# Strassen steps for five of eleven gate/up pairs, and a feed-forward in four interleaved parts

## The chip, the core and the metric

The program runs on one core of one Trainium2 chip. The metric is the device time of one execution in microseconds (us). TensorE (PE in the profile) multiplies, VectorE (DVE), ScalarE (ACT) and GpSimd (POOL) compute elementwise, and SyncE (SP) issues the loads. Each engine works through its own list of instructions in order; semaphores make one engine wait for another.

## The reference, cut to what matters

One transformer layer with 256 rows and a model width of 2048 in float32. Attention, retention and gates come first and are not touched by the change. What follows them is the feed-forward:

```python
h2 = rms_norm(x, g_ffn)
g, u = jnp.split(h2 @ w_ffn_in, 2, axis=-1)     # w_ffn_in: 2048 x 11264, gate and up halves of 5632
return x + (jax.nn.silu(g) * u) @ w_ffn_out     # w_ffn_out: 5632 x 2048
```

## The kernel before, in words

Activations are stationary in TensorE (128 rows of K on the partitions, 128 tokens as columns), and the weights stream past them 512 columns at a time. The 256 tokens are two blocks of 128. Every float32 operand is split into two parts, hi and lo, in the type float32r; a product is three matmuls, hi by hi, hi by lo and lo by hi (`mm3`, L85 to L89).

The weights are one long stream. A *chunk* is 512 columns of a weight matrix over all of K, and adds into two PSUM banks, one for each token block (tag `pm`, four banks, so that one chunk's pair can be emptied while the next chunk's fills). A *group* is two tiles of 128 rows of K of a chunk: 2 tiles x 2 token blocks x 3 = 12 matmuls. For a group, ACT writes the hi part of 128 x 1024 weights (`wh`, L79) and DVE subtracts it from the raw weights to get the lo part (`wl`, L80). Hi and lo have four buffers each, and the split of a group stands three groups ahead of its matmuls (`SPLIT_AHEAD`). A raw tile (`raw`, 1 MB, three buffers) holds two groups; SP issues its load (L135) when a buffer comes free, and that is when DVE has subtracted the last group in it.

When a chunk ends, it is evacuated. A gate chunk goes through ACT's Silu (L544), an up chunk through two DVE instructions that multiply it by the gate (L552). The hidden block is then transposed by DVE in 16 STREAM_TRANSPOSE instructions and split in two halves; `later` spreads these over the next eight groups (L277 to L290).

The feed-forward is eleven pairs of a gate and an up chunk (16 tiles of K each). After six of them come four chunks of `w_ffn_out` (w_fo) over the hidden width made so far, after the other five four more (L592 to L598). All of it is written in program order; the Tile scheduler fixes, before the run, the order of the instructions on each engine and which buffer a tile gets.

Of the kernel before, what the change touches and what calls it, by code (L numbers as in the profile page):

```python
# [39 lines left out]
def hybrid_layer_kernel(ctx, tc, xt, x, w_in, w_oa, w_or, w_out, qg, kg, gm, gf, w_fi, w_fo, out):  # L40
    """One token block of 256 rows through the layer.

    Every float32 operand of a product is split exactly into two parts of 12 significant bits
    (float32r), and a product is hi*hi + hi*lo + lo*hi in float32 accumulation. Activations are
    stationary (K on partitions), weights stream past them 512 columns at a time. RMS scales
    multiply the products' rows, gains multiply the transposed activations' rows. VectorE transposes
    activations in 32 x 32 blocks, which leaves TensorE to the products.
    """
# [42 lines left out]
    def rsqrt(a, w):  # L91
        """1/sqrt(a), with a Newton step after the table's square root; a is overwritten."""
# [11 lines left out]
    chunks = []  # L104
    groups = []

    def add_chunk(w, cols, kts, lhs, evac, before=None):
        ci = len(chunks)
        chunks.append(dict(w=w, cols=cols, kts=kts, lhs=lhs, evac=evac, before=before))
        j = 0  # L110
        while j < len(kts):
            # The first tiles are small, so that the products start early.
            n = 1 if ci == 0 and j < FIRST else SPLIT_KT
            i = j - j % LOAD_KT
            groups.append(dict(c=ci, first=(j == 0), last=(j + n >= len(kts)), load=i, off=j - i, n=n, j=j))
            j += n

    raws = {}

    def emit_load(g):  # L120
        G = groups[g]
        C = chunks[G["c"]]
        key = (G["c"], G["load"])
        if key in raws:
            return
        kts = C["kts"][G["load"]:G["load"] + LOAD_KT]
        t = wp.tile([P, LOAD_KT, NC], F32, tag="raw", bufs=3, name=nm("raw"))
        step = groups[g]["n"] if G["c"] == 0 else LOAD_KT
        for k in range(0, len(kts), step):
            kk = kts[k:k + step]  # L130
            n = len(kk)
            c0 = 0
            for a, ln in C["cols"]:
                src = C["w"][kk[0] * P:(kk[0] + n) * P, a:a + ln].rearrange("(k p) n -> p k n", p=P)
                nc.sync.dma_start(t[:, k:k + n, c0:c0 + ln], src)  # L135
                c0 += ln
            if G["c"] == 0:
                load_xt(G["load"] + k, n)
        raws[key] = t

    parts = {}

    def emit_split(g):
        G = groups[g]
        t = raws[(G["c"], G["load"])]
        hi = wp.tile([P, SPLIT_KT, NC], F32R, tag="hi", bufs=SPLIT_AHEAD + 1, name=nm("wh"))
        lo = wp.tile([P, SPLIT_KT, NC], F32R, tag="lo", bufs=SPLIT_AHEAD + 1, name=nm("wl"))
        n = G["n"]
        split(hi[:, 0:n, :], lo[:, 0:n, :], t[:, G["off"]:G["off"] + n, :])
        parts[g] = (hi, lo)  # L150

    acc = {}

    def emit_mm(g):
        G = groups[g]
        C = chunks[G["c"]]
        if G["first"]:
            acc[G["c"]] = [ps.tile([P, NC], F32, tag="pm", bufs=4, name=nm("pm")) for _ in range(NB)]
        hi, lo = parts.pop(g)
        n = G["n"]  # L160
        for b in range(NB):
            o = acc[G["c"]][b]
            bs = slice(b * P, (b + 1) * P)
            for i in range(n):
                lh, ll = C["lhs"](C["kts"][G["j"] + i])
                mm3(o, (lh[:, bs], ll[:, bs]), (hi[:, i, :], lo[:, i, :]),
                    start=G["first"] and i == 0, stop=G["last"] and i == n - 1)
# [21 lines left out]
    # Idle work while the first tiles come in: ScalarE's table, TensorE's clock.  # L189
# [37 lines left out]
    def build_consts():  # L227
# [4 lines left out]
        # rel[p, :128] = p - j in the first block of rows, rel[p, 128:] = 128 + p - j in the second.  # L232
# [6 lines left out]
        # dec[j, h, i] = exp(log_g[h] * (i - j)) for i >= j, else 0.  # L239
# [420 lines left out]
```

## Time and profile before

| | us |
|---|---|
| median of 3 runs (1545.41 to 1546.79) | 1546.36 |
| span of the profiled execution | 1543.8 |
| median less the span (what lies around it) | 2.6 |
| TensorE busy | 1535.9 |
| VectorE busy | 1045.1 |
| ScalarE busy | 723.2 |

The span runs from the first to the last instruction of the profiled execution; its own time as a run is not listed, so the difference from the median stands for what lies around it. The busy times are sums of instruction durations. An engine that is busy all the time is the first candidate for what sets the end, but whether the others keep up is read stage by stage.

### The profile page before, as it was taken

The page shows a single profiled execution, that of the slowest core. Times are in us where ns is not written, and L with a number is a line of the kernel's source. Part 1 is how long each engine was busy: PE and PEld are TensorE (multiplying, and loading weights), DVE is VectorE, ACT ScalarE, POOL GpSimd, SP SyncE. Part 2 cuts the span into 40 slices and gives each one's busy share as a digit, 9 for nine tenths or more (in the row PEclk, how much of TensorE's full clock was granted, in tenths as well). Part 3 has the DMA queues.
Part 4 walks back from the last instruction along what each step waited for, and adds up shares of the span by engine and source line. Part 5 has one row for each costly group of instructions (what it writes and reads, how often), then busy time and mean ns, then how long its engine had stood idle before and what let it go on. Part 6 is the DMA issues. An engine that isn't in the chain of part 4 may idle for free.

```text
span 1543.8 us, 17497 instructions
## 1 busy us (share of the span) xinstructions
PE 1535.9 (99%) x6837; PEld 1270.3 (82%) x6837; DVE 1045.1 (68%) x1424; ACT 723.2 (47%) x827; POOL 21.1 (1%) x28
## 2 busy tenths in 40 slices
PE   9999999999999999999999999999999999999998
PEld 6788888888888888888888888888888888888887
DVE  7989868777764747474998666666744466666743
ACT  7565554545454444444455444444433444444432
POOL 1101000000000000000000000000000000000000
PEclk9999999999999999999999999999999999999999
DMA  9455555565566555566556655655656555655663
GB/s 351 167 191 163 171 183 192 164 197 185 173 199 196 195 191 191 191 210 228 189 192 197 204 185 194 201 191 191 192 192 196 196 185 193 209 192 191 204 204 109
DMA packets 157907, 298.95 MB, mean 194 GB/s; under 512 B 5216, under 2 KB 22144, under 8 KB 157568
## 3 DMA queue, kind: packets, MB, share of 16 engines
q1 hardware_dynamic: 157696, 297.82, 58.4%
q8 instruction: 53, 0.87, 0.2%
q14 instruction: 30, 0.25, 0.0%
q0 software_dynamic: 128, 0.02, 0.0%
HBM read 295.72 MB, written 2.10 MB: 193 GB/s over the span
## 4 chain that ended last, share of the span: by engine, by line
PE 98%; DVE 1%; DMA 0%; issue 0%; ACT 0%; SPq 0%; ACTq 0%; DVEq 0%
PE pm L88 32%; PE pm L89 32%; PE pm L87 32%; PE sd L88 1%; PE sd L89 1%; PE sd L87 0%; DVE e L290 0%; DVE wl L80 0%; DMA raw<-in_w_in 0%; PE sd L372 0%; SPq L205 0%; SPq L135 0%; ACT L95 0%; ACT wh L79 0%; DVE e L569 0%
## 5 line engine op out<-in xcount | busy, mean ns | idle before, releaser
L80 DVE TENSOR_TENSOR wl<-raw,wh 128x1024 fp32r<-128x1024 f32 (+1 forms) x554 | 673.9, 1220 | 448.8 <-ACT wh L79 444.9
L79 ACT ACTIVATE wh<-raw 128x1024 fp32r<-128x1024 f32 (+1 forms) x554 | 583.3, 1056 | 685.4 <-PE pm L89 660.7
L87 PE MATMUL pm<-wh,u 128*128 128x512 f32 x2208 | 860.3, 390 | 1.5 <-ACT u L82 0.8
L88 PE MATMUL pm<-wl,u 128*128 128x512 f32 x2208 | 859.2, 389 | 1.2 <-DVE wl L80 1.1
L89 PE MATMUL pm<-wh,u 128*128 128x512 f32 x2208 | 859.1, 389 | 0.0
L87 PEld LDWEIGHTS pm<-wh,u 128*128 128x128 f32 x2208 | 414.5, 188 | 89.0 <-ACT u L82 2.6
L88 PEld LDWEIGHTS pm<-wl,u 128*128 128x128 f32 x2208 | 414.6, 188 | 87.4 <-DVE wl L80 2.1
L89 PEld LDWEIGHTS pm<-wh,u 128*128 128x128 f32 x2208 | 414.5, 188 | 86.3 <-DVE u L83 0.2
L290 DVE STREAM_TRANSPOSE e<-e 32x256 f32<-32x256 f32 x432 | 188.3, 436 | 11.4 <-ACT e L400 3.9
L79 ACT ACTIVATE u<-e 128x512 fp32r<-128x512 f32 x50 | 29.0, 625 | 49.9 <-DVE e L290 49.9
L80 DVE TENSOR_TENSOR u<-e,u 128x512 fp32r<-128x512 f32 x50 | 32.7, 691 | 0.5 <-ACT u L79 0.5
L290 DVE STREAM_TRANSPOSE e<-u 32x256 f32<-32x256 f32 x64 | 27.9, 436 | 1.3
L544 ACT ACTIVATE e<-pm,rstd 128x512 f32<-128x512 f32 x22 | 15.1, 690 | 9.3 <-PE pm L89 9.2
L344 POOL TENSOR_SCALAR e<-rel 128x384 f32<-128x384 f32 x8 | 14.1, 1766 | 114.9 <-PE sd L372 33.9
L552 DVE SCALAR_TENSOR_TENSOR e<-pm,rstd,e 128x512 f32<-128x512 f32 x22 | 15.4, 743 | 0.0
L82 ACT ACTIVATE u<-e,g_ffn 128x256 fp32r<-128x256 f32 x16 | 7.2, 498 | 15.1 <-DVE e L290 15.1
L475 ACT ACTIVATE e<-pm,rstd 128x512 f32<-128x512 f32 x16 | 10.9, 690 | 6.6 <-PE pm L89 6.6
L569 DVE TENSOR_TENSOR e<-pm,u 128x512 f32<-128x512 f32 x8 | 5.2, 684 | 7.9 <-PE pm L89 7.9
L95 ACT ACT_TABLE_LOAD x8 | 10.3, 1283 | 0.1
L483 DVE TENSOR_TENSOR e<-pm,e 128x512 f32<-128x512 f32 x16 | 10.2, 682 | 0.0
L362 ACT ACTIVATE e<-e,s 128x128 f32<-128x128 f32 (+1 forms) x16 | 7.2, 448 | 5.4 <-DVE s L359 5.4
L460 DVE TENSOR_TENSOR e<-e,e 128x1024 f32<-128x1024 f32 x4 | 4.9, 1224 | 5.7 <-ACT e L459 5.7
(111 smaller groups left out, 292.9 us busy)
## 6 DMA issues: line engine op xcount, KB each, us to landing
raw<-in_w_fi SPq DMA_DIRECT2D x88, 1024.0 KB, 4.9
raw<-in_w_in SPq DMA_DIRECT2D x84, 1024.0 KB, 5.0
raw<-in_w_fo SPq DMA_DIRECT2D x44, 1024.0 KB, 5.1
raw<-in_w_in SPq DMA_DIRECT2D x38, 512.0 KB, 4.3
raw<-in_w_or SPq DMA_DIRECT2D x16, 1024.0 KB, 5.1
raw<-in_w_out SPq DMA_DIRECT2D x16, 1024.0 KB, 5.0
raw<-in_w_oa SPq DMA_DIRECT2D x8, 1024.0 KB, 5.1
u<-in_x SPq DMA_DIRECT2D x4, 1024.0 KB, 7.4
```

Of the source, the lines that this page charges most:

```text
L79: nc.scalar.activation(hi, src, AF.Copy)
L80: nc.vector.tensor_tensor(lo, src, hi, op=ALU.subtract)
L87: nc.tensor.matmul(o, lh, rh, start=start, stop=False)
L88: nc.tensor.matmul(o, lh, rl, start=False, stop=False)
L89: nc.tensor.matmul(o, ll, rh, start=False, stop=stop)
L95: nc.scalar.activation(r, a, AF.Sqrt)
L290: nc.vector.transpose(o[:, :, :, q, :], i[:, :, :, f * 32:(f + 1) * 32])
L344: nc.gpsimd.tensor_scalar(bias, rel, -(0.5 ** (hh + 1)), None, op0=ALU.mult)
L475: nc.scalar.activation(t[:, b, :], pm[b], AF.Sigmoid, scale=rstd[:, b:b + 1])
L483: nc.vector.tensor_tensor(t[:, b, :], pm[b], t[:, b, :], op=ALU.mult)
L544: nc.scalar.activation(t[:, b, :], pm[b], AF.Silu, scale=rstd2[:, b:b + 1])
L552: nc.vector.scalar_tensor_tensor(t[:, b, :], pm[b], rstd2[:, b:b + 1], t[:, b, :], op0=ALU.mult, op1=ALU.mult)
```

## The change

Five of the eleven gate/up pairs (all but `PLAIN`) are made by one Strassen step. The two token blocks and the two halves of K make a 2 x 2 block matrix of the activations, A11 to A22; the two halves of K and the gate and up columns make one of the weights, B11 to B22. Seven block products replace eight. Each needs a sum of weight blocks or of activation blocks:

- On the activations, four sum forms S1 to S4 are made once, for all pairs, when x1 is transposed (`sum_forms`).
- On the weights, DVE makes the sums anew for each tile of K, in place in the raw tile: one 128 x 1024 addition before the first group and two 128 x 512 additions after the second (`split_` in `strassen`).
- A Strassen pair is 4 groups of 6 matmuls for the product P = A11 B11, whose weights are loaded a first time for it, and then 8 times a triple of groups of 6 matmuls, for the six other products. These accumulate in the four banks of tag `sd` and in two of `pm`. That is 168 matmuls for a pair, against 192.
- At its end seven DVE additions combine the seven products (`ev_gu`), with Silu on ACT between.

A heavy group (6 matmuls) needs a split of the same size as a plain one (12 matmuls), and the sums on top. So the stream is mixed: the feed-forward has four parts of 3, 3, 3 and 2 pairs, and `mixed` spreads a part's plain chunks and the w_fo chunks of the part before between its heavy groups. Pairs 1; 3 and 5; 7; 10 are the Strassen pairs of the four parts. Part 2 has 56 heavy groups and 40 plain ones. The w_fo products of the last part end the kernel.

Tag `e` has five buffers for six, and the constants of the attention are released before the feed-forward, which leaves room for two more hidden tiles.

```diff
+PARTS = (3, 3, 3, 2)
+PLAIN = (0, 2, 4, 6, 8, 9)
...
+    def strassen(w, ca, cb, evac):
...
+        def load(kk):
...
+            t = raw_tile((ci, "m", kk))
+            for slots, c in ((slice(0, 4, 3), ca), (slice(1, 3), cb)):
+                r = k1(kk) * P
+                nc.sync.dma_start(t[:, slots, :], w[r:r + 3 * P, c:c + NC].rearrange("(k p) n -> p k n", p=P)[:, 0:3:2, :])
+
+        def split_(kk, g):
+
+            t = raws[ci, "m", kk]
+            hi, lo = st[kk, g] = wparts()
+            if g == 0:
+                nc.vector.tensor_tensor(t[:, 0:2, :], t[:, 0:3:2, :], t[:, 1:2, :].to_broadcast([P, 2, NC]), op=ALU.add)
+                split(hi, lo, t[:, 2:4, :])
+            elif g == 1:
+                split(hi, lo, t[:, 0:2, :])
+                nc.vector.tensor_tensor(t[:, 0, :], t[:, 0, :], t[:, 2, :], op=ALU.add)
+                nc.vector.tensor_tensor(t[:, 1, :], t[:, 0, :], t[:, 3, :], op=ALU.add)
+            else:
+                split(hi, lo, t[:, 0:2, :])
+
+        def mm(kk, g):
...
+            todo = ((("S4", "T"), ("A12", "Y")), (("S1", "W"), ("S3", "V")), (("S2", "X"), ("A22", "Z")))[g]
+            for i, (a, x) in enumerate(todo):
+                mm3(st[x], lhs_s(a, kk), (hi[:, i, :], lo[:, i, :]), start=kk == 0, stop=kk == NK // 2 - 1)
...
+    def ev_gu(j):
+
+        def f(st):
+            c = st["c"]
+            sl = pair()
+            h = pair()
+            nc.vector.tensor_tensor(c[:, 1, :], st["X"], c[:, 0, :], op=ALU.add)
+            nc.vector.tensor_tensor(sl[:, 0, :], st["Y"], c[:, 0, :], op=ALU.add)
+            nc.scalar.activation(sl[:, 0, :], sl[:, 0, :], AF.Silu, scale=rstd2[:, 0:1])
+            nc.vector.tensor_tensor(h[:, 1, :], st["V"], c[:, 1, :], op=ALU.add)
+            nc.vector.tensor_tensor(c[:, 1, :], st["W"], c[:, 1, :], op=ALU.subtract)
+            nc.vector.tensor_tensor(sl[:, 1, :], st["Z"], h[:, 1, :], op=ALU.add)
+            nc.scalar.activation(sl[:, 1, :], sl[:, 1, :], AF.Silu, scale=rstd2[:, 1:2])
+            nc.vector.tensor_tensor(h[:, 0, :], st["T"], c[:, 1, :], op=ALU.add)
+            nc.vector.tensor_tensor(h[:, 1, :], st["W"], h[:, 1, :], op=ALU.subtract)
+            for b in range(NB):
+                nc.vector.scalar_tensor_tensor(h[:, b, :], h[:, b, :], rstd2[:, b:b + 1], sl[:, b, :], op0=ALU.mult, op1=ALU.mult)
+            hidden(j, h)
...
-    HALF = 6
-    for j0, j1 in ((0, HALF), (HALF, NJ)):
-        for j in range(j0, j1):
-            add_chunk(w_fi, one(j * NC), K, lhs_x1, ev_g(j))
-            add_chunk(w_fi, one(FF + j * NC), K, lhs_x1, ev_u(j))
-        for n in range(4):
-            add_chunk(w_fo, one(n * NC), list(range(4 * j0, 4 * j1)), lhs_hid, ev_fo(n, j1 == NJ))
...
+    j0 = 0
+    fo = []
+    for p in PARTS + (0,):
+        heavy, light = [], []
+        for j in range(j0, j0 + p):
+            if j in PLAIN:
+                light += plain(w_fi, one(j * NC), K, lhs_x1, ev_g(j)) + plain(w_fi, one(FF + j * NC), K, lhs_x1, ev_u(j))
+            else:
+                heavy += strassen(w_fi, j * NC, FF + j * NC, ev_gu(j))
+        groups += mixed(heavy, light + fo, 8 if j0 == 0 else 0, 8 if j0 + p == NJ and p else 0)
+        fo = []
+        for n in range(4):
+            fo += plain(w_fo, one(n * NC), list(range(4 * j0, 4 * (j0 + p))), lhs_hid, ev_fo(n, j0 + p == NJ))
+        j0 += p
```

How the order moves on DVE, first in the steady run of the feed-forward. Before, inside a plain chunk, DVE has nothing but subtractions (`wl`), one for each 12 matmuls:

```order
L80 TENSOR_TENSOR wl_8317<-raw_8175,wh_8316 128x1024
L80 TENSOR_TENSOR wl_8337<-raw_8175,wh_8336 128x1024
L80 TENSOR_TENSOR wl_8355<-raw_8212,wh_8354 128x1024
L80 TENSOR_TENSOR wl_8373<-raw_8212,wh_8372 128x1024
L80 TENSOR_TENSOR wl_8389<-raw_8252,wh_8388 128x1024
```

Now, in part 2, a plain tile (raw_7415) and a Strassen tile (raw_7435) alternate; `wlo` are the lo parts, L231, L235 and L236 the sums in the raw tile:

```order
L92 TENSOR_TENSOR wlo_7563<-raw_7415,whi_7562 128x1024
L231 TENSOR_TENSOR raw_7435<-raw_7435 128x1024
L92 TENSOR_TENSOR wlo_7573<-raw_7435,whi_7572 128x1024
L92 TENSOR_TENSOR wlo_7590<-raw_7435,whi_7589 128x1024
L92 TENSOR_TENSOR wlo_7604<-raw_7415,whi_7603 128x1024
L235 TENSOR_TENSOR raw_7435<-raw_7435 128x512
L236 TENSOR_TENSOR raw_7435<-raw_7435 128x512
L92 TENSOR_TENSOR wlo_7623<-raw_7435,whi_7622 128x1024
L92 TENSOR_TENSOR wlo_7633<-raw_7523,whi_7632 128x1024
L231 TENSOR_TENSOR raw_7543<-raw_7543 128x1024
```

A cycle of 42 matmuls (three heavy groups, two plain) has five subtractions, a wide sum and two narrow ones. The loads on SP alternate in the same way: the Strassen tile raw_7543 takes the buffer of the plain tile raw_7415 and can be issued once wlo_7604 is made; the plain tile raw_7523 has the buffer of the Strassen tile before raw_7435.

Second, on DVE, the end of the first Strassen pair (pair 1), which is also the end of pair 2's up chunk; e_6680 is P, the `sd` and `pm` tiles are the six other products, pm_7154 and pm_7155 the up chunk:

```order
L92 TENSOR_TENSOR wlo_7340<-raw_7235,whi_7339 128x1024
L702 TENSOR_TENSOR e_6680<-pm_6708,e_6680 128x512
L92 TENSOR_TENSOR wlo_7356<-raw_7235,whi_7355 128x1024
L705 TENSOR_TENSOR e_7366<-pm_6709,e_6680 128x512
L685 SCALAR_TENSOR_TENSOR e_7132<-pm_7154,rstd_105,e_7132 128x512
L706 TENSOR_TENSOR e_6680<-sd_6706,e_6680 128x512
L707 TENSOR_TENSOR e_7365<-sd_6707,e_7366 128x512
L709 TENSOR_TENSOR e_7366<-sd_6705,e_6680 128x512
L710 TENSOR_TENSOR e_7366<-sd_6706,e_7366 128x512
L712 SCALAR_TENSOR_TENSOR e_7366<-e_7366,rstd_105,e_7365 128x512 x2
L92 TENSOR_TENSOR wlo_7381<-raw_7265,whi_7380 128x1024
L685 SCALAR_TENSOR_TENSOR e_7132<-pm_7155,rstd_105,e_7132 128x512
```

Before, the end of an up chunk put two such instructions (L552) between the subtractions and 16 transposes behind them. Here eleven stand around four subtractions, and 32 transposes (two hidden blocks) follow among the next seven. TensorE has 6832 rows in the order before and 6712 now.

## Rows read from the trace of the kernel before

**Rows 1.** The page: busy shares, TensorE's clock by slice, and the chain.
```profile
PE 1535.9 (99%) x6837; PEld 1270.3 (82%) x6837; DVE 1045.1 (68%) x1424; ACT 723.2 (47%) x827; POOL 21.1 (1%) x28
...
PEclk9999999999999999999999999999999999999999
...
PE 98%; DVE 1%; DMA 0%; issue 0%; ACT 0%; SPq 0%; ACTq 0%; DVEq 0%
```

**Rows 2.** Timeline: start, duration (a matmul's is modelled); two matmuls twelve apart.
```profile
899.79 0.39 PE L87 MATMUL pm<-wh,u 128*128 128x512 f32 x1
...
902.51 0.39 PE L87 MATMUL pm<-wh,u 128*128 128x512 f32 x1
```

**Rows 3.** Waits in total: engine, line, releaser; us, times, longest.
```profile
ACT wh L79 <- PE pm L89: 660.7, 424, 2.4
DVE wl L80 <- ACT wh L79: 444.9, 329, 3.0
SPq L135 <- DVE wl L80: 1249.2, 252, 8.2
```

**Rows 4.** Timeline: one release passing from ACT to DVE, idle before in brackets.
```profile
900.67 1.06 ACT L79 ACTIVATE wh<-raw 128x1024 fp32r<-128x1024 f32 x1 [1.66 <-PE pm L89]
...
901.76 1.23 DVE L80 TENSOR_TENSOR wl<-raw,wh 128x1024 fp32r<-128x1024 f32 x1 [1.50 <-ACT wh L79]
```

**Rows 5.** Busy us by stretch of the feed-forward: PE, PEld, DVE, ACT, POOL, clock, DMA.
```profile
822.00:1132.00 310.00, 310.00 (x1369) 256.76 (x1369) 206.58 (x266) 140.04 (x150) 0.00 (x0) 1.00 0.59 194
...
sum 721.80, PE 717.83 PEld 594.24 DVE 441.81 ACT 307.48 POOL 0.00; mean PE 179.46 PEld 148.56 DVE 110.45 ACT 76.87 POOL 0.00
```

**Rows 6.** Groups of the feed-forward (822.00 to the end): count, busy us, mean ns.
```profile
L80 DVE TENSOR_TENSOR wl<-raw,wh 128x1024 fp32r<-128x1024 f32 x261 | 319.2, 1223 | 265.0 <-ACT wh L79 263.5
L290 DVE STREAM_TRANSPOSE e<-e 32x256 f32<-32x256 f32 x176 | 76.7, 436 | 3.4
L552 DVE SCALAR_TENSOR_TENSOR e<-pm,rstd,e 128x512 f32<-128x512 f32 x22 | 15.4, 743 | 0.0
L80 DVE TENSOR_TENSOR u<-e,u 128x512 fp32r<-128x512 f32 x22 | 14.2, 685 | 0.0
L569 DVE TENSOR_TENSOR u<-pm,u 128x512 f32<-128x512 f32 x8 | 5.1, 682 | 0.0
L79 ACT ACTIVATE wh<-raw 128x1024 fp32r<-128x1024 f32 x261 | 276.6, 1060 | 376.1 <-PE pm L89 375.6 <-ACT e L518 0.5
```

**Rows 7.** Groups of the whole span, nearest to what is new in the change.
```profile
L320 DVE TENSOR_TENSOR e<-e,rr 128x1024 f32<-128x1024 f32 x2 | 2.4, 1222 | 0.1
L87 PE MATMUL sd<-u,pt 128*128 128x512 f32 x12 | 4.8, 398 | 0.0
L87 PE MATMUL pm<-wh,u 128*128 128x512 f32 x2208 | 860.3, 390 | 1.5 <-ACT u L82 0.8 <-ACT wh L79 0.7
```

**Rows 8.** Timeline of DVE around the ends of up chunks.
```profile
914.87 1.78 DVE L290 STREAM_TRANSPOSE e<-e 32x256 f32<-32x256 f32 x4
916.69 1.23 DVE L80 TENSOR_TENSOR wl<-raw,wh 128x1024 fp32r<-128x1024 f32 x1
...
923.10 1.29 DVE L80 TENSOR_TENSOR u<-e,u 128x512 fp32r<-128x512 f32 x2
924.30 1.22 DVE L80 TENSOR_TENSOR wl<-raw,wh 128x1024 fp32r<-128x1024 f32 x1
...
950.72 1.23 DVE L80 TENSOR_TENSOR wl<-raw,wh 128x1024 fp32r<-128x1024 f32 x1 [1.49 <-ACT wh L79]
951.87 1.40 DVE L552 SCALAR_TENSOR_TENSOR e<-pm,rstd,e 128x512 f32<-128x512 f32 x2
```

**Rows 9.** DMA issues: count, KB each, median us from issue to landing.
```profile
raw<-in_w_fi SPq DMA_DIRECT2D x88, 1024.0 KB, 4.9
...
raw<-in_w_in SPq DMA_DIRECT2D x38, 512.0 KB, 4.3
```

**Rows 10.** TensorE at the start: nine matmuls (ns min/median/max; first, last start).
```profile
L196 PE MATMUL sd<-zero x9: 607/634/634, 1.2 to 4.6; 128*128 128x512 bf16 x9
```

More of the change, by code (lines that the diff above doesn't have):

```diff
@@ new lines, in rows, with plain, load, split_ @@
+    def rows(w, kts, a, ln):
+        return w[kts[0] * P:(kts[0] + len(kts)) * P, a:a + ln].rearrange("(k p) n -> p k n", p=P)
+    def plain(w, cols, kts, lhs, evac, before=None):
+        ci = nm("c")
+        st = {}
+        begin = not groups
+        out_groups = []
+        def load(i):
+            if (ci, i) in raws:
+                return
+            t = raw_tile((ci, i))
+            step = 1 if begin and i < FIRST else SPLIT_KT if begin else LOAD_KT
+            n_all = len(kts[i:i + LOAD_KT])
+            for k in range(0, n_all, step):
+                kk = kts[i + k:i + min(k + step, n_all)]
+                c0 = 0
+                for a, ln in cols:
+                    nc.sync.dma_start(t[:, k:k + len(kk), c0:c0 + ln], rows(w, kk, a, ln))
+                    c0 += ln
+                if begin:
+                    load_xt(kk[0], len(kk))
+        def split_(j, n):
+            if begin:
+                for k in range(n):
+                    split_xt(j + k)
+            hi, lo = st[j] = wparts()
+            o = j % LOAD_KT
+            split(hi[:, 0:n, :], lo[:, 0:n, :], raws[ci, j - o][:, o:o + n, :])
+        def mm(j, n):
+            if j == 0:
+                if before:
+                    before()
+                st["acc"] = [ps.tile([P, NC], F32, tag="pm", bufs=4, name=nm("pm")) for _ in range(NB)]
+            hi, lo = st.pop(j)
+            for b in range(NB):
+                bs = slice(b * P, (b + 1) * P)
+                for i in range(n):
+                    lh, ll = lhs(kts[j + i])
+                    mm3(st["acc"][b], (lh[:, bs], ll[:, bs]), (hi[:, i, :], lo[:, i, :]),
+                        start=j + i == 0, stop=j + i == len(kts) - 1)
+            if j + n == len(kts):
+                evac(st.pop("acc"))
@@ L110, in add_chunk @@
         j = 0
         while j < len(kts):
-            n = 1 if ci == 0 and j < FIRST else SPLIT_KT
-            i = j - j % LOAD_KT
-            groups.append(dict(c=ci, first=(j == 0), last=(j + n >= len(kts)), load=i, off=j - i, n=n, j=j))
+            n = 1 if begin and j < FIRST else SPLIT_KT
+            out_groups.append((lambda i=j - j % LOAD_KT: load(i), lambda j=j, n=n: split_(j, n), lambda j=j, n=n: mm(j, n)))
             j += n
[L118 to L167, printed above, removed]
+        return out_groups
@@ L169, in hybrid_layer_kernel, with mixed @@
+    def mixed(a, b, lead, tail):
+        r = b[:lead]
+        k = 0
+        b, end = b[lead:len(b) - tail], b[len(b) - tail:]
+        for i, g in enumerate(a):
+            r.append(g)
+            while k < len(b) and (k + 1) * len(a) <= (i + 1) * len(b):
+                r.append(b[k])
+                k += 1
+        return r + b[k:] + end
     jobs = []
@@ L602, in hybrid_layer_kernel @@
         for gg in range(g, min(g + LOAD_AHEAD, NG)):
-            emit_load(gg)
-        if g < NG and groups[g]["c"] == 0:
-            for i in range(groups[g]["n"]):
-                split_xt(groups[g]["j"] + i)
+            groups[gg][0]()
         if g == 5:
@@ L613, in hybrid_layer_kernel @@
         if g < NG:
-            emit_split(g)
+            groups[g][1]()
         m = g - SPLIT_AHEAD
@@ L618, in hybrid_layer_kernel @@
         now[0] = m
-        G = groups[m]
-        C = chunks[G["c"]]
-        if G["first"] and C["before"]:
-            C["before"]()
-        emit_mm(m)
-        if G["last"]:
-            C["evac"](acc.pop(G["c"]))
+        if m == n_mix - 8:
+            att_scope.close()
+            extra.append(ctx.enter_context(tc.tile_pool(name="extra", bufs=1)))
+        groups[m][2]()
         run_jobs(m)
```

136 lines of the change are left out of this document (106 added, 30 removed).

## The prediction, made before the changed kernel was run

> **What bounds the kernel now.** I began with the page's busy shares and its chain of waits. TensorE is busy 99% of the span and holds 98% of the chain, at full granted clock in all slices [rows 1]. The timeline gives its pace: matmuls twelve apart start 2.72 us apart, 0.2267 us each [rows 2]. The waits say that the others follow TensorE: ACT's split waits for TensorE to free a buffer (660.7 us in all), DVE's waits for ACT's, SP's loads wait for DVE's [rows 3]. A release runs through this line without loss: ACT starts at 900.67 and takes 1.06, DVE starts at 901.76 [rows 4]. So fewer matmuls are worth 0.2267 us each, as long as DVE, the next engine, keeps up. In the feed-forward DVE is busy 441.81 us of 721.80, ACT 307.48 [rows 5].
>
> **What is removed.** Five pairs have 168 matmuls for 192, so 120 fewer: 120 x 0.2267 = 27.2 us. The feed-forward's 3168 matmuls (718.2 us) become 3048 (691.0 us). Matmuls that change their bank every third time are not in the trace. The nearest rows are the 398 ns of those into the `sd` banks against 390 ns [rows 7]. The columns streamed are the same, so nothing is gained; the dearer end is 8 ns for 840 matmuls, 6.7 us. I take nought, the modelled ends being no pace.
>
> **What DVE gets.** All by its kind [rows 6]:
> - 28 subtractions for a Strassen pair in place of 16: 60 more, 1.223 each, 73.4 us.
> - 40 wide sums. One operand is read twice by broadcast; L320 does that in 1.222 us [rows 7]: 48.9 us. 80 narrow sums by the 0.685 of a 128 x 512 subtraction: 54.8 us.
> - 35 additions at pair ends, 0.682: 23.9 us. 16 more additions for w_fo in four parts instead of two: 10.9 us.
>
> That is 212 us, and 442 + 212 = 654 us of DVE against 691 of TensorE: 95%, where it was 61%. ACT gets 60 splits of 1.06, 64 us more, and stays near 54%. The mean therefore still leaves TensorE ahead. The parts do not: their mixtures differ.
>
> Back to back, DVE starts the next instruction a little before the end of the last: 1.15 from a subtraction to the next instruction, 0.70 for L552, 0.60 for the 128 x 512 subtraction, 0.445 for a transpose, but 1.23 or more where the next has just been released [rows 8]. I use 1.2, 0.72 (L552), 0.70 (additions at pair ends), 0.65 (narrow sums), 0.62 and 0.445.
>
> Part 2 (pairs 3, 4, 5 and the first w_fo products): 56 x 6 + 40 x 12 = 816 matmuls, 185.0 us. DVE, with the ends of pairs 1 to 4 that fall in it: 96 subtractions 115.2, 16 wide sums 19.2, 32 narrow 20.8, two Strassen ends (7 x 0.70 + 2 x 0.72) 12.7, two up ends 2.9, 64 transposes 28.5, 8 hidden subtractions 5.0, 8 w_fo additions 5.6: 210 us. So DVE is the bound there, by 25 us. In the other parts TensorE has more plain groups per heavy one, and DVE has room.
>
> **Where it bites.** The excess does not spread. In a steady cycle (42 matmuls, 9.52 us) DVE has 5 subtractions, 1 wide and 2 narrow sums, 8.5 us, and keeps up. It piles up where a Strassen pair ends, since the additions can't start before TensorE has finished the product X, and the next subtractions are queued behind them on DVE. For those TensorE waits, four buffers of weights being all that DVE may be ahead.
>
> End of pair 1 and of pair 2's up chunk: from the addition of X to the subtraction wlo_7563 DVE has 6 additions 4.2, 4 multiplications 2.9, 32 transposes 14.2, 4 hidden subtractions 2.5, 11 weight subtractions and a wide sum 14.4, 2 narrow sums 1.3: 39.5 us. TensorE has 105 matmuls in hand from the end of X to that group, 23.8 us. It waits 15.7, say 16 us.
>
> End of pair 3: 6 additions and 2 multiplications 5.6, 2 w_fo additions 1.4, 16 transposes 7.1, 2 hidden subtractions 1.2, 10 subtractions and a wide sum 13.2, 2 narrow 1.3: 29.8 us, against 105 matmuls, 23.8: 6 us. Pair 4's up chunk ends just before; its 9.8 us (2 x 0.72, 16 transposes, 2 subtractions) are not worked off at 1 us a cycle, and the additions start some 5 us late: 11 us.
>
> Ends of pairs 5 and 7: 24.9 us by the same count (8 subtractions, no sums) against 91 matmuls, 20.6: 4 us each. Pair 10 ends among plain groups: nothing.
>
> Smaller: four sum forms of the last quarter of x1 stand before its split at the start of the feed-forward, 0 to 4 us, I take 1. Plain chunks have two `pm` banks left, not four, while a Strassen pair runs, so a chunk's first matmuls wait for the one before it to be emptied; a heavy group (1.36 us) stands between, so 0 to 6 us, I take 2, in part 2 alone. Five buffers of `e` for six: up to some waits in the attention, where the engines' order is unchanged; nought, at most 3. The 10 MB that are loaded twice ride on queues at 59% [rows 5].
>
> **The load.** A Strassen tile's load is issued when the plain tile's second subtraction is done and must land before the next wide sum; four DVE instructions close the loop. A 1 MB load takes 4.9 us, a half 4.3 [rows 9]; two halves issued after each other come to about the same. The loop is 4.9 + 4 x 1.2 = 9.7 us against 9.52 of TensorE: 0.2 in each of some 14 cycles, about 2 us, to be had at either end 0 or, if the load takes 6, 18. The Trainium skill (DMA: Bandwidth & Descriptors, Anatomy of one DMA) puts a transfer (there one issued by GpSimd) at a fixed 2.0 us and the bytes over 436 GB/s, 4.4 us for 1 MB: by that the loop would be 9.2, under TensorE's 9.52, and the 2 us would be nought. The rows show 4.9, and I go by them.
>
> **Sum.** -27.2 + 16 + 11 + 4 + 4 + 1 + 2 + 2 = +12.8 us. The profiled span of 1543.8 becomes 1556.6; the median of the runs stands 2.6 above the span, so 1559.2: 1559 us, 0.8% slower.
>
> **Rivals.**
> - *DVE's lead covers the pair ends* (faster). With all four buffers full, about 7 us of TensorE's work, at each pair end, the waits shrink to 9 + 4 + 0 + 0 and the small ones to 3: -27.2 + 16 = -11, 1535 us. It decides from 24 us of waits downwards. For it: the mean load of 95%. Against: X is finished by the last heavy group, so DVE has to wait for TensorE right there and gives up its lead.
> - *Balance*: waits of 24 to 30 us, 1543 to 1549 us, if the ends cost two thirds of my count.
> - *Loads bound every cycle*: at 6 us a load, 1.1 us more in each of 16 cycles of part 2, 18 us: 1577 us. For it: two transfers overlap in the new order, and SP always waits for DVE [rows 3]. Against: the queues are idle 41% of the time.
> - *The clock falls.* The first nine matmuls, after TensorE had done nothing, started 0.43 us apart ((4.6 - 1.2) / 8), 512 columns at 1.2 GHz, though the column of the granted clock says full speed there too [rows 1, 10]. If the starved stretches ran so, their 105 matmuls would take 45 us, above DVE's 39.5 and 34.8: 16 us more, 1575 us. Against: the matmuls come in small lots, with gaps of 1 to 4 us. The Trainium skill (TensorE: Matmul & The Clock Gate, HAM oscillation) warns of such gaps in a kernel that waits for loads; no row here has a gap as long in the middle of the run.
> - *That 120 matmuls don't go*: TensorE has 6712 rows for 6832 in the order. Ruled out.
>
> **Chances.** Forecast 0.60, lead 0.15, balance 0.10, loads 0.10, clock 0.05. A change under 0.2% (3 us) can't be told from none. Faster: the lead's 0.15 and a little of balance, 0.16; same 0.10; slower 0.74. The range goes from 1540, between the lead's 1535 and balance, to 1580, which takes in loads, clock, and the 6.7 us of the banks: some 2 in 10 lie outside.
>
> **What would show it.** In the profile after: a TensorE busy share below 98% with idle time put down to the lo split, almost all in the second quarter of the feed-forward (some 940 to 1090 us); DVE at 9 tenths in those slices; two stretches of 30 to 40 us, after the first and the second Strassen pair, where TensorE is short by 16 and 11 us; steady cycles of 9.5 to 9.8 us between. DVE's sums at 1.22 and 0.69. I am wrong if DVE shows idle time waiting for ACT or TensorE in those stretches while TensorE doesn't wait, or if the loads end the waits.

## The result, and the profile after

The changed kernel takes 1588.26 us (median of 4 runs, 1584.44 to 1589.53) beside 1546.57 us for the kernel before: a ratio of 1.0266, 95% interval [1.0252, 1.0281]. It is 2.7% slower, by 41.7 us. The prediction had the sign, and a loss of 12.8 us; the time lies outside its range.

The page of the changed kernel, the lines that answer to [rows 1]:

```profile
PE 1540.5 (97%) x6717; PEld 1251.0 (79%) x6717; DVE 1244.1 (78%) x1667; ACT 787.1 (50%) x904; POOL 22.8 (1%) x28
...
PEclk9999999999999999999999998998999999999999
...
PE 64%; DVE 22%; DMA 6%; issue 4%; ACT 3%; SPq 0%; ACTq 0%; DVEq 0%
```

TensorE held 98% of the chain and holds 64% now; VectorE (DVE) has 22%. In two of the 40 slices the granted clock is lower. The profiled execution took 1589.53 us, the longest of the four.

Next, TensorE's waits for the other engines, the whole span of the changed kernel: line and what it waited for, us, times, longest. `wlo` and `whi` (L92, L91) are the lo and hi parts of a group's weights, L724 a w_fo addition.

```profile
PE pm L100 <- DVE wlo L92: 20.5, 23, 2.3
PE pm L99 <- ACT whi L91: 8.1, 6, 2.4
PE sd L99 <- ACT whi L91: 5.6, 6, 3.2
PE pm L99 <- DVE u L724: 3.3, 3, 1.6
```

These are some 38 us in all. They don't hold all of the loss, since matmuls that follow a wait run slower (below). The way to all of it is to count: the length of a stretch less its matmuls at 0.2267 us [rows 2]. First the feed-forward as a whole, TensorE's busy time, count and clock, the kernel before:

```profile
820.00:1543.80 723.80, 719.83 (x3176) 1.00 0.58 191
```

and the changed kernel, with the stretches in which it loses time:

```profile
820.00:1587.80 767.80, 724.34 (x3060) 0.98 0.58 195
...
818.00:850.00 32.00, 28.92 (x114) 0.95 0.50 165
900.00:915.00 15.00, 11.39 (x41) 0.89 0.46 142
955.00:1010.00 55.00, 43.36 (x164) 0.88 0.44 152
1055.00:1120.00 65.00, 56.68 (x215) 0.92 0.52 172
1175.00:1210.00 35.00, 32.17 (x138) 1.00 0.59 202
1380.00:1412.00 32.00, 28.98 (x120) 1.00 0.49 166
1455.00:1485.00 30.00, 27.21 (x112) 0.94 0.58 197
```

Before, 723.8 - 3176 x 0.2267 = 3.8 us lost; after, 767.8 - 3060 x 0.2267 = 74.1. So 116 matmuls less in the records give 26.3 us, 70.3 us of new loss take them back, and the 44.0 us between are the whole difference of the two spans. By stretch (a matmul on an edge counts on both sides, some 0.2 us):

| what ends there | predicted loss | lost |
|---|---|---|
| 818 to 850: the feed-forward starts | 1 | 6.2 |
| 900 to 915: pair 0's up chunk | 0 | 5.7 |
| 955 to 1010: pair 1 and pair 2's up chunk | 16 | 17.8 |
| 1055 to 1120: pair 4's up chunk, then pair 3 | 11 | 16.3 |
| 1175 to 1210: pair 5 | 4 | 3.7 |
| 1380 to 1412: pair 7 | 4 | 4.8 |
| 1455 to 1485: pair 9's up chunk | 0 | 4.6 |
| all else | 4 | 15.0, of which 3.8 were there before |

Between the ends little is lost: from 1010 to 1055 us there are 193 matmuls, 43.8 us of 45, and from 1210 to 1300 us 398, all 90.

What such an end looks like, VectorE's timeline at the end of pairs 1 and 2 in the changed kernel (L702 to L712 combine the seven products, L685 multiplies pair 2's up chunk, L410 transposes, L231, L235 and L236 are the wide and narrow sums):

```profile
959.10 0.69 DVE L702 TENSOR_TENSOR e<-pm,e 128x512 f32<-128x512 f32 x1 [0.48 <-PE pm L101]
...
964.49 1.40 DVE L712 SCALAR_TENSOR_TENSOR e<-e,rstd,e 128x512 f32<-128x512 f32 x2
965.81 1.22 DVE L92 TENSOR_TENSOR wlo<-raw,whi 128x1024 fp32r<-128x1024 f32 x1
966.95 0.74 DVE L685 SCALAR_TENSOR_TENSOR e<-pm,rstd,e 128x512 f32<-128x512 f32 x1
...
971.80 3.57 DVE L410 STREAM_TRANSPOSE e<-e 32x256 f32<-32x256 f32 x8
975.40 1.23 DVE L92 TENSOR_TENSOR wlo<-raw,whi 128x1024 fp32r<-128x1024 f32 x1
976.66 3.59 DVE L410 STREAM_TRANSPOSE e<-e 32x256 f32<-32x256 f32 x8
980.27 1.23 DVE L231 TENSOR_TENSOR raw<-raw 128x1024 f32<-128x1024 f32 x1
981.42 1.22 DVE L92 TENSOR_TENSOR wlo<-raw,whi 128x1024 fp32r<-128x1024 f32 x1
...
1000.93 1.23 DVE L231 TENSOR_TENSOR raw<-raw 128x1024 f32<-128x1024 f32 x1 [3.31 <-DMA raw<-in_w_fi]
```

From the addition of X at 959.10, for which VectorE waited, it has no idle time until 997.6 us, 38.5 us; the prediction counted 39.5. From 970 to 986 us a weight subtraction comes only about every 5 us. ScalarE is held by the same engine; its row shows it waiting 2.35 us for the wide sum, with the hi parts behind:

```profile
981.59 2.00 ACT L91 ACTIVATE whi<-raw 128x1024 fp32r<-128x1024 f32 x2 [2.35 <-DVE raw L231]
```

TensorE's timeline in the changed kernel shows what that does:

```profile
982.70 0.79 PE L99 MATMUL sd<-whi,u 128*128 128x512 f32 x1 [3.23 <-ACT whi L91]
983.30 0.63 PE L100 MATMUL sd<-wlo,u 128*128 128x512 f32 x1
983.72 0.63 PE L101 MATMUL sd<-whi,u 128*128 128x512 f32 x1
...
987.60 0.80 PE L100 MATMUL pm<-wlo,u 128*128 128x512 f32 x1 [1.97 <-DVE wlo L92]
988.19 0.63 PE L101 MATMUL pm<-whi,u 128*128 128x512 f32 x1
```

A wait of 3.23 us for that hi part, then matmuls 0.42 to 0.43 us apart, the pace of the nine at the start [rows 10], then another wait.

VectorE does not make up its delay between the ends. In the chain of the changed kernel no matmul stands from 959.1 to 1204.4 us, that is from the end of pair 1 to that of pair 5: there the chain runs through VectorE, and through ScalarE and the loads that wait for it. A piece of the chain after the first large end (start, us, what; `SPq L224` issues the load of a Strassen tile):

```profile
993.01 0.61 DVE raw L236
993.73 1.07 ACT whi L91
994.81 0.37 SPq L224
995.23 5.58 DMA raw<-in_w_fi
1000.93 1.24 DVE raw L231
1002.27 1.07 ACT whi L91
1003.37 2.37 DVE wlo L92 x2
```

The load goes out only when the late split is done with the buffer, and VectorE then waits for it, 3.31 us at 1000.93. Inside a cycle there is a second such turn, the timelines of ScalarE and VectorE: the narrow sum must be made before ScalarE can write the hi part, and VectorE waits for that.

```profile
1017.43 2.01 ACT L91 ACTIVATE whi<-raw 128x1024 fp32r<-128x1024 f32 x2 [2.89 <-DVE raw L236]
...
1018.53 2.36 DVE L92 TENSOR_TENSOR wlo<-raw,whi 128x1024 fp32r<-128x1024 f32 x2 [1.21 <-ACT whi L91]
```

So VectorE's cycles, from one wide sum to the next between 1000.93 and 1059.36 us, take 9.4 to 10.3 us, though its instructions fill only some 8.3 of them. TensorE's cycle takes 9.52 us, and VectorE comes to the next end without a lead.

The start of the feed-forward was not in the prediction. It begins in the output projection, where VectorE's busy time by chunk was, in the kernel before,

```profile
756.00:777.80 21.80, 19.35 (x31) 1.00 0.56 184
777.80:799.60 21.80, 19.40 (x32) 1.00 0.60 194
```

and in the changed kernel, from one addition of a chunk (L637) to the next,

```profile
757.00:780.50 23.50, 21.50 (x34) 1.00 0.52 168
780.50:803.70 23.20, 21.27 (x34) 1.00 0.56 187
803.70:827.20 23.50, 21.50 (x34) 1.00 0.52 174
```

The sum forms add some 2 us a chunk to 19.4 in 21.8, and VectorE waits for ScalarE for 6.0 us in the three. Its work alone would still fit into 21.8; with the waits a chunk takes 23.2 to 23.5. TensorE still needs 21.8 us a chunk, so VectorE stands some 5 us behind it when the feed-forward starts, where it had a lead.

### The profile page after: what moved, and what is told of

Its sections match the earlier page's. It is cut to its first block, busy times and chain, and to the rows that moved or that the text cites. A ratio compares the mean times of both kernels' runs of the same rounds, so it can differ in the third digit from the quotient of the medians.

```text
span 1587.8 us, 17802 instructions
## 1 busy us (share of the span) xinstructions
PE 1540.5 (97%) x6717; PEld 1251.0 (79%) x6717; DVE 1244.1 (78%) x1667; ACT 787.1 (50%) x904; POOL 22.8 (1%) x28
## 4 chain that ended last, share of the span: by engine, by line
PE 64%; DVE 22%; DMA 6%; issue 4%; ACT 3%; SPq 0%; ACTq 0%; DVEq 0%
PE pm L100 20%; PE pm L101 20%; PE pm L99 20%; DVE wlo L92 11%; DVE e L410 6%; DMA raw<-in_w_fi 5%; ACT whi L91 2%; DVE raw L231 1%; PE sd L100 1%; PE sd L101 1%; PE sd L99 1%; DMA raw<-in_w_fo 1%; DVE u L92 1%; DVE raw L235 1%; DVE raw L236 1%
## 5 line engine op out<-in xcount | busy, mean ns | idle before, releaser
L91 ACT ACTIVATE whi<-raw 128x1024 fp32r<-128x1024 f32 (+1 forms) x614 | 637.3, 1054 | 631.8 <-PE pm L101 417.1
L92 DVE TENSOR_TENSOR wlo<-raw,whi 128x1024 fp32r<-128x1024 f32 (+1 forms) x614 | 739.6, 1219 | 268.8 <-ACT whi L91 262.7
L100 PE MATMUL pm<-wlo,u 128*128 128x512 f32 x1912 | 752.8, 394 | 19.4 <-DVE wlo L92 19.2
L99 PE MATMUL pm<-whi,u 128*128 128x512 f32 x1912 | 747.7, 393 | 13.7 <-ACT whi L91 8.1
L101 PE MATMUL pm<-whi,u 128*128 128x512 f32 x1912 | 749.0, 392 | 0.3 <-DVE u L92 0.3
L100 PEld LDWEIGHTS pm<-wlo,u 128*128 128x128 f32 x1912 | 361.6, 189 | 108.3 <-DVE wlo L92 34.1
L99 PEld LDWEIGHTS pm<-whi,u 128*128 128x128 f32 x1912 | 360.7, 189 | 96.6 <-ACT whi L91 15.6
L101 PEld LDWEIGHTS pm<-whi,u 128*128 128x128 f32 x1912 | 361.8, 189 | 75.8 <-DVE u L92 0.7
L410 DVE STREAM_TRANSPOSE e<-e 32x256 f32<-32x256 f32 x432 | 188.3, 436 | 11.0 <-ACT e L520 3.9
L99 PE MATMUL sd<-whi,u 128*128 128x512 f32 x160 | 62.4, 399 | 5.6 <-ACT whi L91 5.6
L100 PE MATMUL sd<-wlo,u 128*128 128x512 f32 x160 | 64.3, 402 | 1.5 <-DVE wlo L92 1.5
L231 DVE TENSOR_TENSOR raw<-raw 128x1024 f32<-128x1024 f32 x40 | 48.9, 1222 | 20.5 <-DMA raw<-in_w_fi 20.4
L101 PE MATMUL sd<-whi,u 128*128 128x512 f32 x160 | 63.5, 397 | 0.0
L91 ACT ACTIVATE u<-e 128x512 fp32r<-128x512 f32 (+1 forms) x56 | 34.5, 654 | 57.3 <-DVE e L410 55.6
L99 PEld LDWEIGHTS sd<-whi,u 128*128 128x128 f32 x160 | 30.3, 191 | 14.7 <-ACT whi L91 8.8
L92 DVE TENSOR_TENSOR u<-e,u 128x512 fp32r<-128x512 f32 (+1 forms) x56 | 39.5, 728 | 0.5 <-ACT u L91 0.5
L101 PE MATMUL pm<-whi,h 128*128 128x512 f32 x96 | 37.4, 390 | 0.0
L99 PE MATMUL pm<-whi,h 128*128 128x512 f32 x96 | 37.0, 391 | 0.1
L101 PEld LDWEIGHTS sd<-whi,u 128*128 128x128 f32 x160 | 30.8, 192 | 6.3
L410 DVE STREAM_TRANSPOSE e<-u 32x256 f32<-32x256 f32 x64 | 27.9, 436 | 1.3
```

The costliest lines, as they stand in the source:

```text
L99: nc.tensor.matmul(o, lh, rh, start=start, stop=False)
L100: nc.tensor.matmul(o, lh, rl, start=False, stop=False)
L101: nc.tensor.matmul(o, ll, rh, start=False, stop=stop)
L231: nc.vector.tensor_tensor(t[:, 0:2, :], t[:, 0:3:2, :], t[:, 1:2, :].to_broadcast([P, 2, NC]), op=ALU.add)
L410: nc.vector.transpose(o[:, :, :, q, :], i[:, :, :, f * 32:(f + 1) * 32])
```

## The experiments

Theory: VectorE's work comes in lumps larger than its lead of three groups, at every chunk's end and in the output projection, and TensorE waits for weights. Rivals: the new order itself, the fallen clock, the loads.

**The order alone**

```diff
-PLAIN = (0, 2, 4, 6, 8, 9)
+PLAIN = tuple(range(11))
...
-            if n % 2 == 0:
-                sT[n // 2] = [unit(shape=(P, 2, 4, 2, P)) for _ in range(2)]
-            transposed(0 if n == 3 else 2, xc, hi[:, k, :], lo[:, k, :], [g_ffn[:, n * 4 + j:n * 4 + j + 1] for j in range(4)],
-                       sums=[t[:, n % 2] for t in sT[n // 2]])
+            transposed(0 if n == 3 else 2, xc, hi[:, k, :], lo[:, k, :], [g_ffn[:, n * 4 + j:n * 4 + j + 1] for j in range(4)])
```

> All eleven pairs plain, no sum forms of x1; the four parts and the w_fo products of a part among the next part's chunks stay. Theory (VectorE is late at the Strassen pairs' ends, and nothing else of the change costs): 3168 matmuls again in the feed-forward, 16 more w_fo additions (10.9 us) hidden, so within 3 us of the kernel before: 1546 to 1550 us. Rival (the new order itself costs: parts, five e buffers instead of six, the h tiles): a third or more of the 69 us lost shows here, 1560 us or more.

1545.18 us, ratio 0.9996 [0.9987, 1.0006]. Four parts, later w_fo products, five `e` buffers and 16 more additions cost nothing that can be measured. All of the loss belongs to the Strassen pairs and what serves them.

**The sums of x1 off VectorE**

```diff
-        nc.vector.tensor_tensor(f[:, 0], a21, a22, op=ALU.subtract)
...
-        split(hi, lo, f)
+        for i, a in enumerate((a11, a21, a12, a22)):
+            nc.scalar.activation(hi[:, i], a, AF.Copy)
+            nc.scalar.activation(lo[:, i], a, AF.Copy)
```

> The four sums of each quarter of x1 and their lo halves are left out of VectorE's work: ScalarE copies x1's blocks in their place, so the Strassen products get wrong left sides. Theory: in the output projection VectorE had 19.6 us of work in 21.8 us before, the sum forms make it 23.2, it falls behind by 1.8 us a chunk and enters the feed-forward with no lead; without them the 6.2 us lost at the start of the feed-forward (818 to 850 us) go, 1582 us. Rival (my predicted 1 us for the sums, the rest of that loss comes from something else): 1587 us.

1589.78 us, 1.0281 [1.0266, 1.0296]: no gain. This run doesn't decide. Its eight copies stand on ScalarE ahead of the hi parts, and VectorE's wait for ScalarE in the same stretch (757 to 827 us) went from 6.0 to 12.8 us; the additions of the chunks are 23 us apart as before. Work was moved, not taken away.

**x1 transposed by TensorE**, which takes it away from VectorE:

```diff
-            transposed(0 if n == 3 else 2, xc, hi[:, k, :], ...
+            transposed_pe(1 if n == 3 else 2, xc, hi[:, k, :], ...
...
+                    nc.tensor.transpose(t[:, c:c + P], tok[:, b, (2 * i + k) * P:(2 * i + k + 1) * P], ident)
```

> The four quarters of x1 are transposed by TensorE instead of VectorE (32 products of 128 columns, some 3.5 us; 28 us less of VectorE in the output projection and at the start of the feed-forward); the feed-forward is as in the changed kernel. Theory (VectorE, with 23.2 us a chunk in the output projection, enters the feed-forward late): its additions stand at 21.8 us apart again and the 6.2 us lost from 818 to 850 us go to about 1: 1586 us. Rival (it is not VectorE's work there but something that stays, the chain of ScalarE's scaled copies): 1590 us or more.

1583.43 us, 1.0242 [1.0227, 1.0258], 4 to 5 us less than the changed kernel, by ratio or by time. TensorE's row for the start of the feed-forward, now without a gap (114 matmuls above; eight of these are short transposes):

```profile
818.00:850.00 32.00, 32.00 (x146) 1.00 0.58 196
```

The additions are 22.72 us apart: TensorE's 21.76 and eight transposes, 0.12 us each. So the 6.2 us came from the output projection. The run takes away VectorE's transposes, and with them the wait for ScalarE behind them; it does not part the two.

**The pair ends transposed by TensorE**

```diff
+    def hidden(j, t, pe=False):
...
+        if pe:
+            transposed_pe(4, t, hid[j][:, 0], hid[j][:, 1], gap=2)
+            return
```

> The hidden chunk of each Strassen pair is transposed by TensorE (8 products of 128 columns with the identity into two sd banks, split from there) in place of VectorE's 16 transposes; plain chunks keep theirs. Theory (VectorE's lump of work at the pair ends): 7.1 us less of VectorE at each end, so pairs 1+2 give back 7, pair 3 some 7, pairs 5 and 7 their 3.7 and 4.8; TensorE gets 40 transposes, at the 0.11 us apart that 128 columns took at 92.83 and 92.94 us in the trace of before, 4.4 us: 1568 to 1574 us. Rival (the additions that wait for X, or the loads, and not the lump): 1586 us or more.

1566.37 us, 1.0132 [1.0117, 1.0147]: 21 to 22 us less. At the two large ends

```profile
955.00:1010.00 55.00, 50.08 (x204) 0.94 0.55 184
1055.00:1120.00 65.00, 57.65 (x244) 1.00 0.58 194
```

there are 204 and 244 matmuls (eight of them short transposes in each) where there were 164 and 215.

**The transposes spread**

```diff
-            later(d + f, transposed_rows, tok, raw, f)
+            later(d + step * f, transposed_rows, tok, raw, f)
...
+        transposed(2, t, hid[j][:, 0], hid[j][:, 1], step=3 if j < 10 else 1)
```

> The four steps of a hidden chunk's transposes come three groups apart instead of one, for pairs 0 to 9; nothing is added or removed. Theory (VectorE's work comes in a lump of 7 to 25 us at a chunk's end, larger than its lead): the ends of pairs 0, 5, 7 and 9, where VectorE has room afterwards, lose little (5.7 + 3.7 + 4.8 + 4.6 us now), those of pairs 1+2 and 3/4 lose less (17.8 + 16.3 now): 1568 to 1576 us. Rival (the loads, or the mean load of VectorE in part 2, bound): 1584 us or more.

1571.24 us, 1.0162 [1.0147, 1.0177]: 17 us less with the same instructions. So at least these 17 us of the loss come from lumps, not from the sum of VectorE's work. The two large ends got back some 3 us each (179 and 227 matmuls in their stretches, where there were 164 and 215); most of the rest came back at the smaller ends, where VectorE has room afterwards (900 to 915 us: 57 for 41, 1380 to 1412 us: 139 for 120).

**TensorE kept busy after two ends**

```diff
+    def zeros(b):
+        if now[0] <= zeros_until[0]:
+            for _ in range(5):
+                nc.tensor.matmul(b, zero[:, 0:P], zero, start=False, stop=False)
```

> In the ten groups after the ends of pairs 1 and 3, five matmuls of a zero tile by a zero tile are added to a bank ahead of each group's own (some 100 in all, 23 us of TensorE if nothing hid them), so that TensorE works while it waits for the lo split. Theory A (the fallen clock has a cost of its own): the granted clock stays at 1.0 in these stretches, and the slow matmuls' loss there, about 9 of 13 us, comes back: 1578 to 1584 us. Theory B (VectorE sets the pace there, and a slow matmul only fills time in which TensorE would have waited): no gain, 1588 us, up to 10 us more where the zeros aren't hidden.

1585.9 us, 1.0257 [1.0241, 1.0272], 1 to 2 us less, and the two intervals overlap. The clock did rise:

```profile
955.00:1010.00 55.00, 47.28 (x193) 0.97 0.47 157
1055.00:1120.00 65.00, 58.14 (x240) 1.00 0.51 165
```

from 0.88 and 0.92. The trace has 56 of the zero matmuls, fewer than announced, and they run before the wait, not through it: at 981.44 us TensorE still waited 2.08 us and ran slowly after. Of the 193 and 240 matmuls 28 in each are zeros. That leaves 165 and 212 of the kernel's own, where 164 and 215 ran in the changed kernel: nothing came back in these stretches. The slow matmuls (starts 0.36 to 0.52 us apart, each less 0.2267) lose by that count 6.3 us there in the changed kernel (the expectation had 9), and 4.5 here. This is theory B for the two large ends, but a gain of a microsecond or two could be covered by zeros that were not hidden. What this execution gained lies ahead of the zeros, where the kernels do not differ; half of it at the start of the feed-forward, 122 matmuls from 818 to 850 us at a clock of 1.00, for 114 at 0.95 in the changed kernel's. The profiled executions of spread3 and pe_ends have 121 and 122 there, also at 1.00, so of the 6.2 us some 1.5 to 2 come and go with the clock from one execution to the next.

**Narrow sums on GpSimd**

```diff
-                nc.vector.tensor_tensor(t[:, 0, :], t[:, 0, :], t[:, 2, :], op=ALU.add)
-                nc.vector.tensor_tensor(t[:, 1, :], t[:, 0, :], t[:, 3, :], op=ALU.add)
+                nc.gpsimd.tensor_tensor(t[:, 0, :], t[:, 0, :], t[:, 2, :], op=ALU.add)
+                nc.gpsimd.tensor_tensor(t[:, 1, :], t[:, 0, :], t[:, 3, :], op=ALU.add)
```

> The 80 narrow sums of weight blocks (0.69 us each, 54.8 us in all) are done by GpSimd instead of VectorE. Theory A (GpSimd works beside VectorE): 1.4 us less of VectorE in each heavy cycle, 2.6 to 4 us back at each of four pair ends and some between: 1572 to 1580 us. Theory B (they get in each other's way): VectorE's subtractions and GpSimd's sums lengthen while they overlap, and little is won: 1586 us or more, with the mean of a 128 x 1024 subtraction above 1.22 us. The Trainium skill (SBUF - State Buffer, Who interferes with whom) says that a VectorE instruction with two inputs in SBUF and a GpSimd instruction that reads SBUF block each other; that is theory B.

1617.39 us, 1.0464 [1.0447, 1.0481]: some 30 us worse than the changed kernel. The groups of this kernel, busy us, mean ns and the idle time before:

```profile
L92 DVE TENSOR_TENSOR wlo<-raw,whi 128x1024 fp32r<-128x1024 f32 x610 | 759.5, 1261 | 321.3 <-ACT whi L91 316.5
L91 ACT ACTIVATE whi<-raw 128x1024 fp32r<-128x1024 f32 x610 | 633.2, 1057 | 659.1 <-PE pm L101 408.1 <-POOL raw L236 117.0 <-DMA raw<-in_w_fi 82.4
L236 POOL TENSOR_TENSOR raw<-raw 128x512 f32<-128x512 f32 x40 | 67.7, 1692 | 3.1
```

The second of two sums that follow each other (L236) takes 1.69 us there for 0.69, and ScalarE waits 117 us for it with the next groups' hi parts behind, where it waited 74.5 us for VectorE's. The subtractions lengthen from 1.222 to 1.261 us, 24 us over 610. The rule of the Trainium skill that the expectation names (SBUF — State Buffer, Who interferes with whom) agrees in direction. How the 30 us divide between the longer subtractions and ScalarE's longer wait is not shown.

**All three together, and fewer pairs.** `v1` joins pe_x1, pe_ends and spread3; `v4_step6` is v1 with `step=6`; the next two differ from v1 in one line:

```diff
-PLAIN = (0, 2, 4, 6, 8, 9)
+PLAIN = (0, 1, 2, 3, 5, 6, 8, 9)      (v2_three_pairs)
+PLAIN = (0, 2, 3, 5, 6, 8, 9)         (v3_four_pairs)
```

> Three things together: TensorE transposes the Strassen pairs' hidden chunks and the quarters of x1, and the plain chunks' transposes come three groups apart. Theory: the lumps are gone but for the additions (7 us, within VectorE's lead of 8 to 11 us) and part 2's mean load of VectorE (210 - 14 = 196 us against 185 + 2 of TensorE); of the 69 us lost 15 to 25 stay, and 72 transposes add 8 us: 1545.4 - 27.2 + 8 + 10 to 25 = 1536 to 1551 us. Rival (the loss has another source in the steady cycles, loads or the two banks): 1560 us or more.

1558.59 us, 1.0079 [1.0062, 1.0096]: 30 us less than the changed kernel, but 8 above the top of the expected range, and not the 1560 of the rival either. Its feed-forward loses 31.7 us with some short transposes among the counted matmuls, and what I took for gone at the ends of pairs 4 and 3 (1040 to 1120 us) is still about 10.

> As v1, the plain chunks' transposes six groups apart instead of three: 1.8 us of VectorE in 16.3 us of TensorE, beside 14.6 of steady work. Theory (lumps): the ends of pairs 0 and 9, 4 each in v1, go to about 1, pairs 1+2 and 4/3 lose somewhat less: 1548 to 1554 us. Rival (mean load in part 2 and five e buffers held longer): 1558 us or more.

1553.76 us, 1.0055 [1.0041, 1.0069], as expected.

> As v1, but pairs 1, 4, 7 and 10 by Strassen. Theory: 96 matmuls less are -21.8; 64 transposes 7; part 1 keeps what it lost in v1 from 880 to 1000 us, some 9.5, part 2 loses like part 3, 2, part 4 4: 1545.7 + 1 = 1544 to 1550 us, 9 to 14 below v1, which has one matmul saving of 5.4 more but the two pairs of part 2 next to each other. Rival (part 2's two pairs don't matter): v1 + 5.4 - 0.9 = 1563 us.

1546.07 us, 1.0000 [0.9991, 1.0009]: one pair less, and 12.5 us faster than v1. Two pairs in part 2 cost more than their matmuls. Whether it is that they follow each other, or that part 2 then has more work for VectorE than time, the run does not part.

> As v1, but only pairs 4, 7 and 10 by Strassen, one for each part that has w_fo products to mix in; part 1 is plain. Theory (what a pair costs depends on VectorE's room in its part): 72 matmuls less are -16.3; 32 + 24 transposes 6; the ends of pairs 4 and 7 1.5 each as pair 7's in v1 (1280 to 1380 us), pair 10's neighbour 9 4: 1545.7 - 3 = 1541 to 1546 us. Rival (each Strassen pair costs more than its 5.4 us wherever it stands): 1548 us or more.

1543.46 us, 0.9980 [0.9971, 0.9989], faster than both kernels by 0.2% and 2.8%. The waits that are left in it:

```profile
PE pm L99 <- DVE u L755: 3.1, 3, 1.5
PE pm L99 <- DVE e L713: 1.6, 1, 1.6
PE sd L300 <- DVE zero L295: 1.2, 1, 1.2
```

For a lo part TensorE waits once, 1.0 us, as before the change. The first two are the two `pm` banks of the plain chunks, emptied late.

> As v2_three_pairs, with the plain chunks' transposes six groups apart and only the last quarter of x1 transposed by TensorE; VectorE transposes the other three. Theory: 24 transposes less of TensorE, 0.12 us each by the 22.72 us between the additions of the output projection in pe_x1 against 21.76, are -2.9; pair 9's end, 3 to 4 us in v2_three_pairs, goes to 1 to 2; VectorE enters the feed-forward 3 x 1.8 us late, but part 1 is plain and gives it room, 0 to 3 us: 1538 to 1542 us. Rival (the late start costs its 5 us whatever follows it): 1543 us or more.

1545.1 us, 0.9996 [0.9987, 1.0005]: the theory's 1538 to 1542 missed, the rival held. The trace says why; three of the quarters on VectorE bring back 23.2 to 23.5 us a chunk, and TensorE's first transpose of the last quarter waits for the late addition (L665):

```profile
827.82 0.33 PE L401 MATMUL sd<-ident,u 128*128 128x128 f32 x1 [2.48 <-DVE u L665]
```

That is VectorE's lag at the start of the feed-forward, seen from TensorE; the six-group spacing did not shorten pair 9's end either (its wait for L713 is 2.6 us, for 1.6).

## Why the prediction was wrong in size

- *What bounds the kernel* held: TensorE, as long as VectorE keeps up.
- *What is removed*: 120 matmuls, 27.2 us. Right; no price for changing banks was seen (398 matmuls in 90 us from 1210 us on).
- *What VectorE gets*: 654 us of 691 forecast for the feed-forward, 641.7 measured from 820 us to the end. The wide sum took 1.222 us, as the broadcast row said [rows 7].
- *Ends of pairs 1 and 2, of 5 and of 7*: 16, 4 and 4 forecast, 17.8, 3.7 and 4.8 lost. VectorE's count against the matmuls in hand fits these ends, and the first is borne out by the 38.5 us of VectorE without a pause.
- *Up chunks that end inside a mixture* are the first step that failed, a term put at nothing. I let the ends of pairs 0 and 9 cost nothing and pair 4's only delay pair 3's additions by 5 us. But the prediction's own 9.8 us of such an end, beside 8.5 of steady work in every 9.52, are above the lead as well: 5.7 and 4.6 us were lost, and TensorE waits from 1069 us on for pair 4's, before pair 3's additions at 1079.89; 16.3 for 11. Spreading the transposes, which takes nothing away, gave 17 us.
- *The steady cycle* is why such an end weighs more than the prediction allowed: it counted VectorE's 8.5 us back to back, so that VectorE would work off 1 us in each 9.52, though its own load loop of 9.7 us stood against that. While VectorE was late its cycles took 9.4 to 10.3 us, with waits for ScalarE (1.21 us in a cycle) and for loads, and it worked off nothing from pair 1's end to pair 5's. This rests on the trace; no run took these waits away.
- *The sum forms*, forecast at 1 us, are the second: 6.2. I looked at the last quarter alone. VectorE had 19.4 us of work in the 21.8 of an output-projection chunk, which the prediction did not count; 2 us more and 2 us of waiting for ScalarE made 23.2 to 23.5, so the three earlier quarters had already spent its lead. pe_x1 took the loss away, v7 brought it back.
- *Two banks and the load loop*, 2 each: waits for `pm` banks of 3.3 us for L724 are in the rows. VectorE waits 20.4 us for loads at L231 in 17 places; in v2_three_pairs it waits 25.9 us there and TensorE hardly at all, so such a wait need not reach TensorE. But in the changed kernel ScalarE also waits 85.4 us for loads of `w_fi`, and the loads hold 6% of the chain, 0% before: the loop holds in the cycles after the ends, in which VectorE should have caught up. The loads go out late there because the split is late; what quicker loads or a fourth raw buffer would give back is open, since no run changed the loads themselves.
- *The clock* was a rival at 0.05 and 16 us. It did fall, to 0.88 over a stretch of 55 us, and slow matmuls lose 11.8 us from 820 us on. At the two large ends all of that loss, or all but a microsecond or two, fills time in which TensorE would have waited: with the clock at 0.97 and 1.00 nothing came back there. At the start of the feed-forward some 1.5 to 2 us hang on it; for pairs 0 and 9 it is not settled. The Trainium skill (TensorE: Matmul & The Clock Gate, HAM oscillation) warned of waits after which TensorE starts slowly. The trace agrees in kind, with waits for the split and not for loads: 3.23 and 1.97 us long, and slow matmuls from 982.70 and from 987.60 us.
- *The lead covers the ends* (1535) was the rival on the fast side. The ends were not covered.
- The sum: 40 us of loss forecast, 70 found. The named stretches hold 23 of the missing 30; some 7 are small losses spread over the rest, not taken apart. So the price of two terms was put at nothing or too low, and the range, which ended at 1580, had no room for either.

## What to carry to other kernels

A counted mean load of 95% on the second engine says little; count its work at every chunk's end against the matmuls that its lead covers, plain chunks and the stage before included, and take its pace from the waits inside a cycle, not from the sum of its instructions. A step that saves matmuls pays only where the engine that feeds it has room: three pairs among plain and w_fo chunks, with the lumps spread, gained 0.2%, a fourth in the part without w_fo products gave it back, and a fifth, the second of its part, cost 12 us. And before taking pairs away, see whether the lump can be spread or given to the engine that waits: 0.96 us of TensorE replaced 7.1 us of VectorE.

## What was not expected of the hardware

- TensorE transposes 256 tokens x 512 columns in 8 x 0.12 us, by the spacing of 22.72 against 21.76 us in pe_x1.
- Some waits of 2 to 3 us in the middle of the run are followed by matmuls 0.42 to 0.43 us apart (1.2 GHz) for 1 to 5 us, after which they are 0.23 apart again: at 991.15 us after the wait that ended at 987.60. After the wait of 1.67 us that ended at 994.84 they were 0.23 apart from the second on.
- A 128 x 512 addition takes GpSimd 1.60 to 1.69 us and VectorE 0.69, and VectorE's subtractions were 3% longer in that kernel.
